# Hybrid trunk on one core: six of eight Mamba-2 groups projected in token rows, and their scans begun five steps later

## The chip, the core and the metric

The kernel runs on one core of one Trainium2 chip. The metric is the device time of one execution in microseconds. Five engines work side by side, each with its own queue in order: TensorE (PE, with its weight loads PEld) for matrix products into PSUM, VectorE (DVE), ScalarE (ACT), GpSimd (POOL), which here only issues transfers, and SyncE (SP), which issues the weight loads. PSUM is the memory that TensorE writes its sums to; SBUF is the large on-chip memory; HBM is off the chip. A partition is one of the 128 rows of SBUF or PSUM.

## The reference

One decoder layer with 256 tokens of width 2048, in float32: a token mixer of two parallel branches (HGRN2 and Mamba-2), cross-attention to 256 memory tokens, and a convolved gated feed-forward. The change lies in the Mamba-2 branch. Cut to what matters:

```python
proj = u @ w_in                        # 2048 -> z, xbc, dt and the rest
xbc = silu(causal_dwconv(xbc_raw, conv_w, conv_b))   # 4 taps over the tokens
xs, bm, cm = split(xbc)                # 2048 channels, 8 x 128, 8 x 128
dt = softplus(dt_raw + dt_bias)
y = ssd_chunk_scan(xs * dt, dt * a, bm, cm) + d_skip * xs
y = y * silu(z)                        # then an RMS norm in each of the 8 groups
y_m2 = y @ w_branch_m2
```

There are eight groups. A group has 512 channels of xbc: 256 of xs (four heads of 64), 128 of B and 128 of C. The convolution runs along the tokens, so it wants a channel in a partition and the tokens beside one another.

## The kernel before

**Weights and steps.** All weights are float32 and every product is made from two parts: a weight chunk of 1 MB (`raw`, L144, three buffers, loaded by SP in the fixed list `order`) is cast to `hi` on ScalarE (L130) and the rest `lo` is taken on VectorE (L131), in halves of 1024 columns, each with five buffers (`WB = 5`). Inputs are split in the same way; `s2` holds the mixer's normed input, 16 blocks of 128 channels, each with 256 columns of `hi` and 256 of `lo`. One call of `weights()` is one step: it lets the background work advance (`step()`), casts weights two chunks ahead, and hands out one chunk.

**Two forms of projection.** `project` makes one chunk of 128 output channels in column form, with channels in partitions: per block of input channels one product of 512 columns (`hi` weights with both parts of the input) and one of 256 (`lo` weights with the `hi` input), 32 products a step, into one PSUM tile; `join` (L263, L264) adds its two halves. `project_tok` makes 512 output channels from four chunks in token form, with tokens in partitions: two PSUM tiles, one for each 128 tokens, and 24 products of 512 columns a step; here the weights are the moving operand. There are four such PSUM tiles (`proj`).

**The Mamba-2 stage.** After the z gates and group 0 come the products of the HGRN2 branch, and then groups 1 to 7. Each even group is preceded by four steps of z gates for two groups (`m2_gates`). `m2_project(g)` makes a group's four chunks in column form, joins each into the tile `t` (one buffer) and convolves it (L725, L728) into `sz` (two buffers, shared by name with other stages). A transfer on SP brings the cumulated decays into `vc` (L718).

**The scan.** `m2_scan` is a generator in the background list; each `yield` ends its part in one step, and `pause(n)` lets n steps pass. It applies SiLU to `sz` (L740, L743), turns xs to token rows through HBM (x, into `kq`), builds the decay matrices `e0`, `e1` (L756 to L761), multiplies B and C on TensorE (`misc<-sz`) and masks them (L769, L773), scales x (L777, into `bb`), multiplies (`misc<-e,bb`), adds the skip term (L792), turns the result (`yt`, again `bb`), gates and norms it (L805 to L813), turns it back (`yc`, L817) and splits it into `ym` (L823, L828). To turn is: 32x32 transposes on VectorE (L320) into `yq` (two buffers), four transfers to HBM (L312) and one back, all issued by POOL.

**Order.** A planner orders each engine's instructions: it takes the earliest written one that it holds to be ready. Products of the background are pinned on TensorE behind what was written before them, so they come at their step; work of ScalarE and VectorE can be taken earlier than its step. A tile that has all its buffers taken waits until the last reader of the oldest is done.

**After the groups** come 16 steps of sigmoid gates (`gate`, L836, two of the four in buffers of `sz`) and the 16 steps of the branch product of `ym`, in token form; its step 4 reads groups 6 and 7.

Of the kernel before, what the change touches and what calls it, by code (L numbers as in the profile page):

```python
# [9 lines left out]
F32 = mybir.dt.float32  # L10
# [4 lines left out]
ALU = mybir.AluOpType  # L15
# [4 lines left out]
P = 128  # L20
T = 256
D = 2048
# [4 lines left out]
GROUPS = 8  # L27
# [37 lines left out]
def hybrid_trunk(ctx, tc, xT, memT, par, cst, msk, w_k0, w_ka, w_va, w_hg, w_hv, w_hog, w_ghg, w_bhg, w_dt,  # L65
# [127 lines left out]
    def pause(n):  # L193
        for _ in range(n):
            yield True
# [149 lines left out]
    def pc(name, i=0, n=1):  # L345
        o, _ = PCOLS[name]
        return par_t[:, o + i:o + i + n]
# [356 lines left out]
    def m2_chunk(g, i):  # L704
        return 2 * g + i if i < 2 else (16 + g if i == 2 else 24 + g)
# [9 lines left out]
    def m2_project(g):  # L715
        sz = mp.tile([P, 4, T], F32, name="sz", bufs=2)
        cb = mp.tile([P, 4, T], F32, name="vc", bufs=2)
        nc.sync.dma_start(out=cb, in_=cum_d[4 * g:4 * g + 4, :].partition_broadcast(P))  # L718
        for i in range(4):
            c = m2_chunk(g, i)  # L720
            ps = project(s2)
            raw = mp.tile([P, T], F32, name="t", bufs=1)
            join(mp, ps, raw)
            o = sz[:, i, :]
            V.tensor_scalar(out=o, in0=raw, scalar1=pc("m2_cw", 4 * c + 3), scalar2=pc("m2_cb", c),  # L725
                            op0=ALU.mult, op1=ALU.add)
            for s in range(1, 4):
                V.scalar_tensor_tensor(out=o[:, s:T], in0=raw[:, 0:T - s],  # L728
                                       scalar=pc("m2_cw", 4 * c + 3 - s), in1=o[:, s:T],
                                       op0=ALU.mult, op1=ALU.add)  # L730
        return sz, cb

    def m2_scan(g, sz, cb, zt):
        yield from pause(1 + 2 * (g % 2) if g else 0)

# [517 lines left out]
def _layout(inp):  # L1253
# [5 lines left out]
    swap = np.arange(D).reshape(GROUPS, 2, P // B, B).transpose(0, 2, 1, 3).ravel()  # L1259
    xs = _cols(cut(10240, 2048)).reshape(GROUPS, 2, P, 2048)  # L1260
    b = _cols(cut(12288, 1024))[:, None]
    c = _cols(cut(13312, 1024))[:, None]
    dt = np.zeros((D, P), f)
# [16 lines left out]
    def put(name, a):  # L1280
# [34 lines left out]
        "w_bhg": _toks(inp["w_branch_hg"][0]), "w_dt": _cols(dt),  # L1315
        "w_z": _toks(cut(8192, 2048)[:, swap]), "w_m2": np.concatenate([xs, b, c], 1), "w_gm2": _toks(cut(16416, 2048)),
        "w_bm2": _toks(inp["w_branch_m2"][0]), "w_out": out,
# [23 lines left out]
```

## Time and profile before

| | |
|---|---|
| median of three runs | 2229.68 us (2229.58 to 2229.78) |
| the profiled execution | 2230.02 us, its span 2228.3 us |
| granted TensorE clock | 0.998 |
| busy TensorE, VectorE, ScalarE, POOL | 100%, 74%, 59%, 8% |
| weight chunks of these groups (`raw<-in_w_m`) | 32 loads of 1 MB, 5.0 us to landing |

In the profile's rows `proj<-s,hi` is a product in column form (weights `hi` held, input `s` moving) and `proj<-hi,s` one in token form; L82 is the helper that issues them all. After `|` come busy time and mean of one, and then the engine's idle time before them and what ended it.

### The profile page before, as it was taken

The page shows a single profiled execution, that of the slowest core. Times are in us where ns is not written, and L with a number is a line of the kernel's source. Part 1 is how long each engine was busy: PE and PEld are TensorE (multiplying, and loading weights), DVE is VectorE, ACT ScalarE, POOL GpSimd, SP SyncE. Part 2 cuts the span into 40 slices and gives each one's busy share as a digit, 9 for nine tenths or more (in the row PEclk, how much of TensorE's full clock was granted, in tenths as well). Part 3 has the DMA queues.
Part 4 walks back from the last instruction along what each step waited for, and adds up shares of the span by engine and source line. Part 5 has one row for each costly group of instructions (what it writes and reads, how often), then busy time and mean ns, then how long its engine had stood idle before and what let it go on. Part 6 is the DMA issues. An engine that isn't in the chain of part 4 may idle for free.

```text
span 2228.3 us, 32921 instructions
## 1 busy us (share of the span) xinstructions
PE 2217.3 (100%) x12620; PEld 1890.7 (85%) x12620; DVE 1640.8 (74%) x2660; ACT 1321.2 (59%) x2056; POOL 186.0 (8%) x314
## 2 busy tenths in 40 slices
PE   9999999999999999999999999999999999999998
PEld 8888888888888888888888888888888888888887
DVE  8858888887645779874676766675776776699887
ACT  7567777776545577665456655554554555465554
POOL 0000100110000122220200010001000100100000
PEclk9999999999999999999999999999999999999999
DMA  8655555555655667766676654578666666655654
GB/s 307 235 187 195 184 181 181 182 186 189 228 189 201 225 234 236 229 213 219 228 247 217 219 203 174 180 226 250 214 210 211 225 214 218 213 200 211 220 205 161
DMA packets 100270, 470.45 MB, mean 211 GB/s; under 512 B 29424, under 2 KB 34064, under 8 KB 51088
## 3 DMA queue, kind: packets, MB, share of 16 engines
q1 hardware_dynamic: 69600, 432.36, 54.8%
q0 software_dynamic: 13584, 33.57, 5.3%
q10 hardware_dynamic: 16928, 2.42, 0.6%
q8 instruction: 99, 1.62, 0.3%
q14 instruction: 59, 0.48, 0.1%
HBM read 445.20 MB, written 25.20 MB: 211 GB/s over the span
## 4 chain that ended last, share of the span: by engine, by line
PE 99%; DMA 0%; ACT 0%; SPq 0%; DVE 0%; issue 0%; DVEq 0%; ACTq 0%
PE proj L82 90%; PE misc L82 5%; PE lev L82 4%; DMA raw<-in_w_k 0%; ACT misc L1204 0%; DVE h L1202 0%; PE lev L869 0%; SPq L402 0%; ACT hi L386 0%; SPq L401 0%; DVE c L1221 0%; SPq L405 0%; DVEq L1337 0%; ACT jt L263 0%; PE misc L697 0%
## 5 line engine op out<-in xcount | busy, mean ns | idle before, releaser
L131 DVE TENSOR_TENSOR lo<-raw,hi 128x1024 fp32r<-128x1024 f32 x738 | 896.5, 1222 | 458.8 <-ACT hi L130 425.9
L130 ACT CAST hi<-raw 128x1024 fp32r<-128x1024 f32 x737 | 771.9, 1051 | 546.5 <-PE proj L82 513.0
L82 PE MATMUL proj<-hi,s 128*128 128x512 f32 x2922 | 913.6, 390 | 0.0
L82 PE MATMUL proj<-s,hi 128*128 128x512 f32 x2736 | 645.1, 391 | 1.1 <-ACT hi L386 1.1
L82 PEld LDWEIGHTS proj<-hi,s 128*128 128x128 f32 x2922 | 548.4, 188 | 114.4 <-issue 0.7
L82 PEld LDWEIGHTS proj<-s,hi 128*128 128x128 f32 x2736 | 506.5, 188 | 101.8 <-ACT hi L386 1.6
L82 PE MATMUL proj<-lo,s 128*128 128x512 f32 x1461 | 568.8, 389 | 0.0
L82 PEld LDWEIGHTS proj<-s,lo 128*128 128x128 f32 x2736 | 345.3, 191 | 11.3 <-ACT s L278 0.8
L82 PE MATMUL proj<-s,lo 128*128 128x256 f32 x2736 | 351.6, 283 | 0.2 <-ACT s L278 0.2
L82 PEld LDWEIGHTS proj<-lo,s 128*128 128x128 f32 x1461 | 274.4, 188 | 55.7
L312 POOL DMA_DIRECT2D x_d<-yq x120 | 69.9, 589 | 372.2 <-DVE yq L320 365.6
L165 ACT CAST hi<-raw 128x1024 fp32r<-128x1024 f32 (+1 forms) x56 | 52.1, 944 | 55.0 <-DVE raw L174 35.1
L263 ACT COPY jt<-proj 128x256 f32<-128x256 f32 x123 | 45.6, 371 | 57.5 <-PE proj L82 56.8
L312 POOL DMA_DIRECT2D u_d<-yq x44 | 28.6, 656 | 535.9 <-DVE yq L1051 342.6
L312 POOL DMA_DIRECT2D y_d<-yq x64 | 35.1, 555 | 384.1 <-DVE sm L618 263.1
L166 DVE TENSOR_TENSOR lo<-raw,hi 128x1024 fp32r<-128x1024 f32 (+1 forms) x56 | 60.2, 1088 | 6.9 <-ACT hi L165 6.2
L1074 DVE SCALAR_TENSOR_TENSOR gc<-g,par_t,gc 128x255 f32<-128x255 f32 x88 | 42.4, 482 | 8.7 <-ACT gc L1072 6.0
L728 DVE SCALAR_TENSOR_TENSOR sz<-t,par_t,sz 128x255 f32<-128x255 f32 (+2 forms) x96 | 45.6, 475 | 1.4
L1072 ACT ACTIVATE gc<-g,par_t 128x256 f32<-128x256 f32 x44 | 26.4, 601 | 20.9 <-DVE g L1070 20.9
L82 PE MATMUL proj<-hi,ha 128*128 128x512 f32 x104 | 36.6, 389 | 0.0
L572 DVE TENSOR_TENSOR e<-e,kq 128x256 f32<-128x256 f32 x96 | 34.4, 418 | 0.0
L559 DVE TENSOR_TENSOR e<-bb 128x256 f32<-128x256 f32 x96 | 33.8, 419 | 0.1
(315 smaller groups left out, 1801.3 us busy)
## 6 DMA issues: line engine op xcount, KB each, us to landing
raw<-in_w_uv SPq DMA_DIRECT2D x44, 1024.0 KB, 4.9
raw<-in_w_ug SPq DMA_DIRECT2D x44, 1024.0 KB, 4.8
raw<-in_w_dn SPq DMA_DIRECT2D x44, 1024.0 KB, 4.8
raw<-in_w_hg SPq DMA_DIRECT2D x32, 1024.0 KB, 4.8
raw<-in_w_m SPq DMA_DIRECT2D x32, 1024.0 KB, 5.0
raw<-in_w_hv SPq DMA_DIRECT2D x16, 1024.0 KB, 4.9
raw<-in_w_hog SPq DMA_DIRECT2D x16, 1024.0 KB, 4.8
raw<-in_w_ghg SPq DMA_DIRECT2D x16, 1024.0 KB, 4.8
```

Of the source, the lines that this page charges most:

```text
L82: ins = PE.matmul(*args, **kwargs)
L130: S.copy(out=hi[:, c - a:d - a], in_=raw[:, c:d])
L131: V.tensor_tensor(out=lo[:, c - a:d - a], in0=raw[:, c:d], in1=hi[:, c - a:d - a].bitcast(F32), op=ALU.subtract)
L165: S.copy(out=hi[:, 0:d - c], in_=raw[:, c:d])
L166: V.tensor_tensor(out=lo[:, 0:d - c], in0=raw[:, c:d], in1=hi[:, 0:d - c].bitcast(F32), op=ALU.subtract)
L263: S.copy(out=tmp, in_=ps[:, T:2 * T])
L312: G.dma_start(out=yd.rearrange("(n i) (b f) -> b i n f", i=B, b=P // B)[b], in_=yq[b * B:(b + 1) * B, :].rearrange("i (n f) -> i n f", n=n))
L559: V.tensor_tensor(out=lev[hw].rearrange("p (n c i) -> p n c i", c=2, i=hw), in0=free(bb, 0, [(2 * hw, nb), (T + hw, 2), (1, hw)]), in1=fre ...
L572: V.tensor_tensor(out=ev, in0=ev, in1=free(kq, 0, [(2 * hw, nb), (T + hw, 2), (1, hw)]), op=ALU.mult)
L728: V.scalar_tensor_tensor(out=o[:, s:T], in0=raw[:, 0:T - s], scalar=pc("m2_cw", 4 * c + 3 - s), in1=o[:, s:T], op0=ALU.mult, op1=ALU.add)
L1072: S.activation(out=gc, in_=g, func=AF.Identity, bias=pc("f_cb", c), scale=pc("f_cw", 3 * c + 2))
L1074: V.scalar_tensor_tensor(out=gc[:, s:T], in0=g[:, 0:T - s], scalar=pc("f_cw", 3 * c + 2 - s), in1=gc[:, s:T], op0=ALU.mult, op1=ALU.add)
```

## The change

Groups 1 to 6 are projected in token form. Their weights are laid out for it on the host (`w_m2`, whose blocks for groups 0 and 7 stay in columns). The two PSUM tiles of a group hold 512 channels in token rows: VectorE transposes them in four operations of 128x256 straight from PSUM into `yq`, POOL sends each of two `yq` to HBM in four transfers and fetches it back in one, into `sz`, which then holds the channels in partitions but with the tokens in another order, not yet convolved. No join is made.

The convolution of these groups moves into their scan. After three steps, ScalarE copies a chunk from `sz` into `t` in the order of the tokens and VectorE convolves it back into `sz`, two chunks in the fourth step and two in the fifth; then the scan goes on with its old pause (1 step for even groups, 3 for odd ones), five steps later than it did. Group 0 is as before. Group 7 is projected as before and its scan begins three steps later (a pause of 6 for 3).

```diff
+        if 0 < g < GROUPS - 1:
+            pss = project_tok(s2)
+            for j in range(2):
+                yq = mp.tile([P, 2 * T], F32, name="yq", bufs=2)
+                for q in range(2):
+                    V.transpose(out=yq.rearrange("p (n q r) -> p q n r", q=2, r=B)[:, q],
+                                in_=pss[q][:, j * T:(j + 1) * T].rearrange("p (n c) -> p n c", c=B))
+                yd = to_squares(yq, T // B, "r_d")
+                G.dma_start(out=sz[:, 2 * j:2 * j + 2, :], in_=yd.rearrange("(i p) t -> p i t", p=P))
+            return sz, cb
         for i in range(4):
-            c = m2_chunk(g, i)
             ps = project(s2)
             raw = mp.tile([P, T], F32, name="t", bufs=1)
             join(mp, ps, raw)
-            o = sz[:, i, :]
-            V.tensor_scalar(...)
-            for s in range(1, 4):
-                V.scalar_tensor_tensor(...)
+            convolve(g, sz, i, raw)
         return sz, cb

+    def convolve(g, sz, i, raw):
+        c = m2_chunk(g, i)
+        o = sz[:, i, :]
+        V.tensor_scalar(out=o, in0=raw, scalar1=pc("m2_cw", 4 * c + 3), scalar2=pc("m2_cb", c),
+                        op0=ALU.mult, op1=ALU.add)
+        for s in range(1, 4):
+            V.scalar_tensor_tensor(out=o[:, s:T], in0=raw[:, 0:T - s],
+                                   scalar=pc("m2_cw", 4 * c + 3 - s), in1=o[:, s:T],
+                                   op0=ALU.mult, op1=ALU.add)

     def m2_scan(g, sz, cb, zt):
-        yield from pause(1 + 2 * (g % 2) if g else 0)
+        if 0 < g < GROUPS - 1:
+            yield from pause(3)
+            for i in range(4):
+                raw = mp.tile([P, T], F32, name="t", bufs=1)
+                S.copy(out=raw.rearrange("p (q b t) -> p q b t", q=2, t=B), in_=in_order(sz[:, i, :]))
+                convolve(g, sz, i, raw)
+                if i % 2:
+                    yield True
+        yield from pause((0, 1, 3, 6)[0 if g == 0 else 3 if g + 1 == GROUPS else 1 + g % 2])
...
+    xbc = np.concatenate([...], 2).reshape(D, GROUPS * 512)
+    m2 = _toks(xbc)
+    for g in (0, GROUPS - 1):
+        m2[g] = _cols(xbc[:, g * 512:(g + 1) * 512])
```

More of the change, by code (lines that the diff above doesn't have):

```diff
@@ L723, in m2_project @@
             join(mp, ps, raw)
-            o = sz[:, i, :]
-            V.tensor_scalar(out=o, in0=raw, scalar1=pc("m2_cw", 4 * c + 3), scalar2=pc("m2_cb", c),
-                            op0=ALU.mult, op1=ALU.add)
-            for s in range(1, 4):
-                V.scalar_tensor_tensor(out=o[:, s:T], in0=raw[:, 0:T - s],
-                                       scalar=pc("m2_cw", 4 * c + 3 - s), in1=o[:, s:T],
-                                       op0=ALU.mult, op1=ALU.add)
-        return sz, cb
-    def m2_scan(g, sz, cb, zt):
-        yield from pause(1 + 2 * (g % 2) if g else 0)
+            convolve(g, sz, i, raw)
+        return sz, cb
+    def convolve(g, sz, i, raw):
[7 more added lines that the diff above has]
+                                   op0=ALU.mult, op1=ALU.add)
+    def m2_scan(g, sz, cb, zt):
+        if 0 < g < GROUPS - 1:
[7 more added lines that the diff above has]
+        yield from pause((0, 1, 3, 6)[0 if g == 0 else 3 if g + 1 == GROUPS else 1 + g % 2])
         xc = mp.tile([P, 2 * T], F32, name=("w", "ql")[g % 2], bufs=1)
@@ L1259, in _layout @@
     swap = np.arange(D).reshape(GROUPS, 2, P // B, B).transpose(0, 2, 1, 3).ravel()
-    xs = _cols(cut(10240, 2048)).reshape(GROUPS, 2, P, 2048)
-    b = _cols(cut(12288, 1024))[:, None]
-    c = _cols(cut(13312, 1024))[:, None]
+    xbc = np.concatenate([cut(10240, 2048).reshape(D, GROUPS, 256),
+                          cut(12288, 1024).reshape(D, GROUPS, P),
+                          cut(13312, 1024).reshape(D, GROUPS, P)], 2).reshape(D, GROUPS * 512)
+    m2 = _toks(xbc)
+    for g in (0, GROUPS - 1):
+        m2[g] = _cols(xbc[:, g * 512:(g + 1) * 512])
     dt = np.zeros((D, P), f)
@@ L1315, in _layout @@
         "w_bhg": _toks(inp["w_branch_hg"][0]), "w_dt": _cols(dt),
-        "w_z": _toks(cut(8192, 2048)[:, swap]), "w_m2": np.concatenate([xs, b, c], 1), "w_gm2": _toks(cut(16416, 2048)),
+        "w_z": _toks(cut(8192, 2048)[:, swap]), "w_m2": m2, "w_gm2": _toks(cut(16416, 2048)),
         "w_bm2": _toks(inp["w_branch_m2"][0]), "w_out": out,
```

## The prediction

> **What bounds the kernel now.** I read the page first: the busy shares, then the chain of waits.
>
> ```profile
> span 2228.3 us, 32921 instructions
> PE 2217.3 (100%) x12620; PEld 1890.7 (85%) x12620; DVE 1640.8 (74%) x2660; ACT 1321.2 (59%) x2056; POOL 186.0 (8%) x314
> ...
> PE 99%; DMA 0%; ACT 0%; SPq 0%; DVE 0%; issue 0%; DVEq 0%; ACTq 0%
> ```
>
> TensorE is busy all the time and the chain of waits is TensorE for 99%. So a change can only gain by making TensorE's stream shorter, and can only lose by making TensorE wait. The profiled execution took 2230.02 us, the median of the runs is 2229.68, so its sum stands 0.34 us above the median.
>
> The same holds inside the stage that is changed. The view of busy time by stretches, for 71 us in its middle (columns: length, then busy time and count of PE, PEld, DVE, ACT, POOL, then clock and DMA):
>
> ```profile
> 778.00:849.00 71.00, 71.00 (x394) 60.88 (x393) 58.06 (x97) 48.85 (x80) 18.05 (x30) 1.00 0.69 232
> ```
>
> 71 us is one period of two groups: 8 steps of their own projection, 4 of the gates z, and two scans. VectorE fills 82% of it, so it has 13 us to spare in two groups and is the engine to watch.
>
> **The gain: 24 steps change their form.** A weight chunk of 1 MB is one step. In column form a step is 16 matmuls of 512 columns and 16 of 256; in token form it is 24 of 512. Both stream 12,288 columns. What a step takes is read from the timeline of PE, first over four column steps without a scan between them, then over a token stretch:
>
> ```profile
> 1150.68 7.44 PE L82 MATMUL proj<-s,hi 128*128 128x512 f32 x32
> 1157.96 4.00 PE L82 MATMUL proj<-s,lo 128*128 128x256 f32 x32
> 1161.80 7.44 PE L82 MATMUL proj<-s,hi 128*128 128x512 f32 x32
> 1169.08 4.00 PE L82 MATMUL proj<-s,lo 128*128 128x256 f32 x32
> 1172.91 2.46 PE L82 MATMUL proj<-s,hi 128*128 128x512 f32 x10
> ```
>
> ```profile
> 1040.35 0.62 PE L82 MATMUL proj<-hi,s 128*128 128x512 f32 x2
> ...
> 1041.03 0.62 PE L82 MATMUL proj<-hi,s 128*128 128x512 f32 x2
> ...
> 1082.51 0.61 PE L82 MATMUL proj<-hi,s 128*128 128x512 f32 x2
> ```
>
> Column form: 1150.68 to 1172.91 is 22.23 us for four steps, 5.558 each. Token form: three matmuls take 0.68 us (1040.35 to 1041.03), and 62 such threes lie between 1040.35 and 1082.51 (42.16 us), so eight threes take 5.440. The difference is 0.118 us, and six groups of four steps give 24 x 0.118 = 2.8 us. The reason shows in the same rows: a matmul of 512 columns comes every 7.28 / 32 = 227.5 ns and one of 256 every 3.84 / 32 = 120.0, which is 0.42 ns a column and some 12.5 ns a matmul whatever its width; token form has eight matmuls fewer per step.
>
> The Trainium skill ("TensorE: Matmul & The Clock Gate", Back-to-back issue gap) gives a warm matmul N / 2.4 + 2.5 ns. By that rule eight matmuls fewer are worth 0.02 us a step, 0.5 us in all. The rows above have five times its fixed part, and I keep to the rows.
>
> **The rest of the edit, engine by engine.** Groups of the stretch 720 to 990 us by line (busy, mean ns, idle before):
>
> ```profile
> L131 DVE TENSOR_TENSOR lo<-raw,hi 128x1024 fp32r<-128x1024 f32 x93 | 112.8, 1221 | 41.7 <-ACT hi L130 39.1 <-PE proj L82 2.2
> L130 ACT CAST hi<-raw 128x1024 fp32r<-128x1024 f32 x92 | 96.3, 1050 | 61.5 <-PE proj L82 61.2
> L312 POOL DMA_DIRECT2D x_d<-yq x84 | 49.0, 589 | 173.7 <-DVE yq L320 168.0 <-DVE sz L725 3.3 <-issue 2.4
> L728 DVE SCALAR_TENSOR_TENSOR sz<-t,par_t,sz 128x254 f32<-128x254 f32 (+2 forms) x83 | 39.3, 474 | 1.0
> L773 DVE TENSOR_TENSOR e<-e,a 128x768 f32<-128x768 f32 x13 | 12.1, 952 | 1.8 <-ACT a L771 1.8
> L264 DVE TENSOR_TENSOR t<-proj,jt 128x256 f32<-128x256 f32 x27 | 11.3, 418 | 2.0 <-ACT jt L263 2.0
> L725 DVE TENSOR_SCALAR sz<-t,par_t 128x256 f32<-128x256 f32 x27 | 11.0, 407 | 0.3
> L263 ACT COPY jt<-proj 128x256 f32<-128x256 f32 x27 | 9.9, 366 | 11.1 <-PE proj L82 11.1
> L777 DVE TENSOR_TENSOR bb<-kq,dt_tok 128x256 f32<-128x256 f32 x14 | 5.6, 417 | 5.7 <-DMA kq<-x_d 5.7
> L750 POOL DMA_DIRECT2D kq<-x_d x7 | 5.0, 721 | 29.9 <-DMA x_d<-yq 29.9
> ```
>
> The operations that this stage doesn't have are bounded by near ones, of the feed-forward part and of the scans:
>
> ```profile
> L1051 DVE STREAM_TRANSPOSE yq<-proj x22: 672/708/718, 1526.4 to 1945.0; 128x512 f32<-128x512 f32 x22
> L320 DVE STREAM_TRANSPOSE yq<-lf x16: 437/445/446, 196.3 to 562.1; 128x256 f32<-128x256 f32 x16
> L823 ACT ACTIVATE s<-yc,par_t x16: 492/495/511, 753.2 to 1027.9; 128x256 fp32r<-128x256 f32 x16
> ```
>
> VectorE, per group: out go four sums of a join, 4 x 418 = 1.7 us. In come four transposes of 128x256 out of PSUM: between half of the 708 ns of twice the width and 445 ns, I take 400, so 1.6 us. The convolutions stay, 407 + 3 x 474 = 1.83 us a chunk. ScalarE: out go four copies of 366 ns, in come four copies out of the reordered buffer, between 366 and 495 ns, I take 430: +0.3 us of some 24 a group. POOL: eight more transfers out at 589 ns and two back at 721, 6.2 us a group on top of 9 (half of the 18.05 above) in 35.5. SP's weight loads and their sizes stay. None of this lies on TensorE; the cover is the lead of the split weights. There are five buffers of half a chunk, so a half is cast when TensorE leaves the one five before it (ScalarE's 61.2 us of waiting for PE above), four halves of 2.72 us ahead of its use: 10.9 - 1.05 - 1.22 = 8.6 us of margin. A stall of ScalarE or VectorE shorter than that costs nothing; what is longer, TensorE pays.
>
> **Waits that are moved.** A scan's products are put into TensorE's order at a step; ScalarE and VectorE take the rest when the planner sees it ready. "Five steps later" thus binds the products, and the results of group 6 and 7 are needed only at the fourth step of the first branch product, 20 steps after group 7's projection, where the last scan now ends 18 steps after it (15 before). Two steps, some 11 us, are left; I cost it at nothing. On SP the transfer of a group's cumulated decays waits for the scan two groups before it, and weight loads queue behind it; such waits cost nothing so far:
>
> ```profile
> SPq L144 <- DVE lo L131: 222.1, 47, 8.8
> ...
> SPq L718 <- ACT e L758: 22.8, 5, 6.9
> ```
>
> The new wait is ScalarE's first copy, which stands in front of weight casts until the turned chunk is back from HBM. The nearest rows are two such hand-overs one behind the other on POOL, and what VectorE did at their end:
>
> ```profile
> 740.21 2.33 POOL L312 DMA_DIRECT2D x_d<-yq  x4 [9.86 <-DVE yq L320]
> 747.82 0.58 POOL L312 DMA_DIRECT2D x_d<-yq  x1 [5.28 <-DVE yq L320]
> 748.43 0.72 POOL L817 DMA_DIRECT2D yc<-x_d  x1
> ...
> 758.30 0.72 POOL L750 DMA_DIRECT2D kq<-x_d  x1 [5.62 <-DMA x_d<-yq]
> ...
> 763.28 0.76 DVE L777 TENSOR_TENSOR bb<-kq,dt_tok 128x256 f32<-128x256 f32 x2 [5.66 <-DMA kq<-x_d]
> ```
>
> A pair took 23 us from the first issue to the use, and VectorE stood 5.66 us without TensorE noticing. The copies come in at the fourth and the fifth step after the group, 3 x 5.44 = 16.3 and 21.8 us. Bounds of what the waits cost: nothing (all below 8.6 us), or, if the planner sets the copies so early that each group's wait is 9.3 us, 6 x 0.7 = 4.2 us. Nearest is the 5.66 us row, so I take nothing.
>
> Sum: 2230.02 - 2.8 = 2227.2 for a profiled execution, 2226.9 against the median; I forecast 2227.0.
>
> **Rivals.** *Late hand-over*: the 4.2 us just priced eat the gain, 2231. For it speaks the 23 us pair, against it that the steps allow nearly as much.
>
> *Group 7 blocked, slower*: the convolved buffer sz has two slots, and group 7 takes that of group 5. Group 5's products, which read it last, move from the 8th to the 13th step after its projection, while group 7 is projected, still in column form, at steps 9 to 12. Its convolutions then start together after step 13, 4 x (0.42 + 1.83) = 9.0 us on VectorE; the single buffer t, held meanwhile, keeps group 6's from running (4 x 1.83 = 7.3), and group 5's own products need 0.42 + 2 x 0.95 + 2 x 0.42 = 3.2. That is 19.5 us at one place. It costs from 8.6 us on, in so far as the planner puts it ahead of the splits, and makes the kernel slower by over 0.2% from 8.6 + 2.8 + 4.5 = 15.9 on. With 17.5 us ahead TensorE waits 8.9: 2235.8, say 2236. Whether splits get in between is seen on VectorE's timeline:
>
> ```profile
> 906.93 0.48 DVE L728 SCALAR_TENSOR_TENSOR sz<-t,par_t,sz 128x255 f32<-128x255 f32 x1
> 907.33 1.22 DVE L131 TENSOR_TENSOR lo<-raw,hi 128x1024 fp32r<-128x1024 f32 x1
> 908.46 0.48 DVE L728 SCALAR_TENSOR_TENSOR sz<-t,par_t,sz 128x254 f32<-128x254 f32 x1
> ...
> 919.82 0.95 DVE L773 TENSOR_TENSOR e<-e,a 128x768 f32<-128x768 f32 x1
> 920.69 0.47 DVE L728 SCALAR_TENSOR_TENSOR sz<-t,par_t,sz 128x254 f32<-128x254 f32 x1
> 921.08 0.95 DVE L773 TENSOR_TENSOR e<-e,a 128x768 f32<-128x768 f32 x1
> ```
>
> At 907 a split runs between two steps of a convolution, which speaks against the rival. At 920 a convolution and a scan alternate and leave no room for one, which speaks for it. While a chain of dependent operations is alone, splits get through; I count on that.
>
> *No gain*: if columns alone set the pace, a step costs the same in both forms, 2229.7. The rows of 227.5 and 120.0 ns speak against it. The skill's rule above is near this case: 2229.2.
>
> *More*: to pass 0.2%, 4.5 us, each of 24 steps would have to save 0.19 us. Only if the change removed some 2 us of small gaps in the stage too, 2224.7; the rows show no gaps that long.
>
> **Chances.** Forecast 0.57, late hand-over 0.17, group 7 blocked 0.17, no gain 0.05, more 0.04. A measurement of this kernel tells about 0.2% from no change, 2225.2 to 2234.1, so a gain of 2.8 us counts as the same: 0.57 + 0.17 + 0.05 = 0.79 same, 0.17 slower, 0.04 faster. The range goes from 2225.6, between forecast and the last case, up to 2234.0, between the two loss cases, and leaves out 0.18.
>
> **What would show it.** The two groups of PE that change, from the page:
>
> ```profile
> L82 PE MATMUL proj<-hi,s 128*128 128x512 f32 x2922 | 913.6, 390 | 0.0
> L82 PE MATMUL proj<-s,hi 128*128 128x512 f32 x2736 | 645.1, 391 | 1.1 <-ACT hi L386 1.1
> ```
>
> Right: the second falls by 384 to 2352, the first rises by 384 to 3306, 192 matmuls are fewer in all (12620 above), PE still 99% of the chain, and the stretch from the first to the last group shorter by 2.8 us. ScalarE's wait for the transfer into sz shows the hand-over, and its cost would be gaps on PE behind a weight cast, once per group. The blocked group 7 would show one gap of several us on PE, some two steps after group 5's products, with convolutions packed on VectorE ahead of it. The prediction is wrong if PE has such gaps, or if the token steps here come slower than 5.44 us.

## The result: 19.1 us slower, and the profile after

Four runs of the changed kernel gave a median of 2248.84 us (2248.52 to 2249.93), against 2229.73 (2229.58 to 2230.13) for the kernel before beside them: 1.0087 times as long (95% interval 1.0074 to 1.0099). The forecast was 2227.0 and the top of the range 2234.0. The profiled execution took 2249.93 us, its span 2248.1, 19.8 more than before.

From the page of the changed kernel:

```profile
span 2248.1 us, 32665 instructions
PE 2222.2 (99%) x12428; PEld 1883.8 (84%) x12428; DVE 1642.7 (73%) x2660; ACT 1331.4 (59%) x2062; POOL 221.8 (10%) x374
...
PE 51%; DMA 0%; issue 0%; ACT 0%; DVE 0%; DVEq 0%; POOLq 0%
...
L82 PE MATMUL proj<-hi,s 128*128 128x512 f32 x3306 | 1034.1, 391 | 3.1 <-ACT s L845 3.1
...
L82 PE MATMUL proj<-s,hi 128*128 128x512 f32 x2352 | 554.5, 390 | 4.2 <-DVE yq L725 3.2
```

The counts of matmuls are those forecast, 192 fewer, and the other engines' busy times have hardly moved (POOL's by 35.8 us). The chain of waits, TensorE for 99% before, can't be compared: here it is followed back only to 1080 us (the shares add up to 51%), and of the stage it says nothing. But the groups of PE now have idle time in front of them. The view of PE's waits says for what (columns: us in total, times, longest):

```profile
PE proj L82 <- ACT sg L712: 7.0, 1, 7.0
PE proj L82 <- DVE yq L725: 3.2, 1, 3.2
PE proj L82 <- ACT s L845: 3.1, 1, 3.1
PE misc L82 <- DVE bb L799: 1.8, 3, 1.4
```

These are 15.1 us. The three large ones have their places in PE's timeline:

```profile
919.78 0.39 PE L82 MATMUL proj<-hi,s 128*128 128x512 f32 x1
927.22 1.44 PE L82 MATMUL proj<-s,lo 128*128 128x256 f32 x5 [7.05 <-ACT sg L712]
928.67 3.07 PE L82 MATMUL misc<-e,bb 128*64 128x256 f32 x16
931.67 2.11 PE L82 MATMUL proj<-s,lo 128*128 128x256 f32 x11
933.61 0.63 PE L82 MATMUL proj<-s,hi 128*128 128x512 f32 x2
...
951.77 1.61 PE L82 MATMUL proj<-s,hi 128*128 128x512 f32 x6 [3.23 <-DVE yq L725]
...
1092.19 0.50 PE L82 MATMUL proj<-hi,s 128*128 128x512 f32 x1 [3.08 <-ACT s L845]
1092.77 0.62 PE L82 MATMUL proj<-hi,s 128*128 128x512 f32 x2
...
1097.10 0.62 PE L82 MATMUL proj<-hi,s 128*128 128x512 f32 x2
```

At 920 TensorE wants a PSUM tile for group 7's first chunk, at 948 one for its fourth, and at 1089 the results of the last scan. After the first and the last gap it is also slow for a while. From 1092.77 to 1097.10 it ran twelve matmuls of 512 columns, which at 227 ns take 2.72 us and took 4.33. From 927.22 to 933.61 it ran sixteen of 256 columns and sixteen small products of a scan in 6.39 us. At 120 ns each, and with the 1.50 us that such products took in the kernel before, that is 3.42:

```profile
922.83 1.57 PE L82 MATMUL misc<-e,bb 128*64 128x256 f32 x16
924.33 0.86 PE L82 MATMUL proj<-s,lo 128*128 128x256 f32 x5
```

The two stretches cost 1.6 and 3.0 us more. The granted clock of the changed kernel in the view by stretches confirms it (last three columns: clock, DMA share, GB/s):

```profile
919.00:932.00 13.00, 5.94 (x28) 4.66 (x27) 6.03 (x12) 9.02 (x16) 0.00 (x0) 0.64 0.37 137
...
1088.00:1098.00 10.00, 6.92 (x23) 5.23 (x23) 5.01 (x10) 2.90 (x4) 0.00 (x0) 0.83 0.47 186
```

The Trainium skill ("TensorE: Matmul & The Clock Gate", What's actually happening) halves TensorE's clock after at least one idle window of about 3.4 us and restores it after about as long a busy one. The trace agrees in the length: the second row is 17% short of 10 us, which at half speed is 3.4 us. It doesn't agree in the threshold: this came after a wait of only 3.08 us, and the 3.23 us at 948 brought none. Even 2.06 us were enough in the run with ScalarE's queue below (clock 0.86 over the 12 us from 915, again 3.4 us at half speed), and a gap of the same 2.06 us was not in the run unread through `yq` (clock 1.00 over the 12 us from 918).

So 15.1 us of waits and 4.6 of half clock, less the forecast gain of 2.8, make 16.9 of the 19.8; the 2.9 us left are in no wait that the view of the stage lists, and are not itemised here.

**What stands behind the gaps.** The PSUM tile at 920 was held by the z gates of groups 6 and 7. Their copy waits for one of the two buffers `sg`, which is free when the gate of group 3 (L827) is done; first VectorE, then ScalarE:

```profile
921.29 1.22 DVE L131 TENSOR_TENSOR lo<-raw,hi 128x1024 fp32r<-128x1024 f32 x1 [0.81 <-ACT hi L130]
922.43 0.41 DVE L740 TENSOR_SCALAR sz<-t,par_t 128x256 f32<-128x256 f32 x1
922.87 1.00 DVE L743 SCALAR_TENSOR_TENSOR sz<-t,par_t,sz 128x255 f32<-128x255 f32 x2
923.79 0.42 DVE L827 TENSOR_TENSOR kq<-bb,sg 128x256 f32<-128x256 f32 x1
...
924.52 0.42 DVE L827 TENSOR_TENSOR kq<-bb,sg 128x256 f32<-128x256 f32 x1
```

```profile
926.60 1.05 ACT L712 COPY sg<-proj 128x512 f32<-128x512 f32 x2
```

The turned result that the gate reads had been fetched by 916.3 us (issued at 912.62, 3.7 us to landing). From there to the gate VectorE was idle for 0.81 us only: it ran splits and the convolutions (L740, L743) of group 5, the late ones.

The tile at 948 was held by group 6's projection, which ended at 920, but whose second pair of transposes runs at 951:

```profile
933.22 1.30 DVE L320 STREAM_TRANSPOSE yq<-kq 128x512 f32<-128x512 f32 x2
...
943.26 0.77 DVE L725 STREAM_TRANSPOSE yq<-proj 128x256 f32<-128x256 f32 x2
951.18 0.77 DVE L725 STREAM_TRANSPOSE yq<-proj 128x256 f32<-128x256 f32 x2
```

Two turns of scans had taken both buffers `yq` at 933, and the projection's pairs came behind them, each only after POOL had sent the older content off. The other two of the four PSUM tiles were held by group 7 itself, by its second and third chunk, whose joins wait for the one buffer `t`:

```profile
938.47 0.42 DVE L264 TENSOR_TENSOR t<-proj,jt 128x256 f32<-128x256 f32 x1 [0.50 <-ACT jt L263]
...
959.90 0.41 DVE L740 TENSOR_SCALAR sz<-t,par_t 128x256 f32<-128x256 f32 x1
...
963.39 0.42 DVE L264 TENSOR_TENSOR t<-proj,jt 128x256 f32<-128x256 f32 x1
```

The first join fills `t` at 938.47. Its convolution into `sz` runs only at 959.90, behind the products of group 5 (957.4) that read the same slot of `sz`, and the second join only after that. POOL waits, in order, for the turns of both kinds (its waits in 730 to 1000 us):

```profile
POOL x_d L312 <- DVE yq L320: 77.0, 12, 16.1
POOL r_d L312 <- DVE yq L725: 42.6, 5, 26.2
POOL sz L728 <- DMA r_d<-yq: 15.8, 7, 4.5
```

The last two rows are new: for 58 us POOL stands in front of the projection's turns. In this kernel no scan's turn of the stage, once transposed, waits more than 2.0 us for its first transfer, as before; what comes late is its transpose. That scans' turns queue behind the projection's on POOL is seen with own buffers (below): a turn transposed at 850.7 us gets its first transfer at 864.8.

### The profile page after: what moved, and what is told of

Read it like the earlier page. It is cut to its first block, busy times and chain, and to the rows that moved or that the text cites. A ratio compares the mean times of both kernels' runs of the same rounds, so it can differ in the third digit from the quotient of the medians.

```text
span 2248.1 us, 32665 instructions
## 1 busy us (share of the span) xinstructions
PE 2222.2 (99%) x12428; PEld 1883.8 (84%) x12428; DVE 1642.7 (73%) x2660; ACT 1331.4 (59%) x2062; POOL 221.8 (10%) x374
## 4 chain that ended last, share of the span: by engine, by line
PE 51%; DMA 0%; issue 0%; ACT 0%; DVE 0%; DVEq 0%; POOLq 0%
PE proj L82 45%; PE misc L82 4%; PE lev L82 3%; DMA yc<-x_d 0%; ACT misc L1226 0%; PE lev L891 0%; DVE h L1224 0%; DVE c L1243 0%; DMA x_d<-yq 0%; ACT s L845 0%; DVEq L1363 0%; ACT r L1233 0%; ACT r L1234 0%; DVE r L1232 0%; POOLq L839 0%
## 5 line engine op out<-in xcount | busy, mean ns | idle before, releaser
L82 PE MATMUL proj<-hi,s 128*128 128x512 f32 x3306 | 1034.1, 391 | 3.1 <-ACT s L845 3.1
L82 PEld LDWEIGHTS proj<-hi,s 128*128 128x128 f32 x3306 | 621.2, 188 | 133.9 <-ACT s L845 3.5
L82 PE MATMUL proj<-lo,s 128*128 128x512 f32 x1653 | 645.2, 390 | 0.0
L82 PE MATMUL proj<-s,hi 128*128 128x512 f32 x2352 | 554.5, 390 | 4.2 <-DVE yq L725 3.2
L82 PEld LDWEIGHTS proj<-s,hi 128*128 128x128 f32 x2352 | 435.0, 188 | 90.8 <-issue 3.6
L82 PEld LDWEIGHTS proj<-lo,s 128*128 128x128 f32 x1653 | 310.8, 188 | 64.5 <-issue 1.5
L82 PEld LDWEIGHTS proj<-s,lo 128*128 128x128 f32 x2352 | 298.1, 192 | 17.2 <-ACT sg L712 7.5
L82 PE MATMUL proj<-s,lo 128*128 128x256 f32 x2352 | 303.8, 284 | 7.0 <-ACT sg L712 7.0
L263 ACT COPY jt<-proj 128x256 f32<-128x256 f32 x99 | 36.7, 371 | 51.2 <-PE proj L82 45.6
L743 DVE SCALAR_TENSOR_TENSOR sz<-t,par_t,sz 128x255 f32<-128x255 f32 (+2 forms) x96 | 46.0, 479 | 1.7
```

Source lines behind the costliest of these rows:

```text
L82: ins = PE.matmul(*args, **kwargs)
L263: S.copy(out=tmp, in_=ps[:, T:2 * T])
L743: V.scalar_tensor_tensor(out=o[:, s:T], in0=raw[:, 0:T - s], scalar=pc("m2_cw", 4 * c + 3 - s), in1=o[:, s:T], op0=ALU.mult, op1=ALU.add)
```

## The experiments

Differences are always to the kernel before, timed beside it (its medians lay between 2229.61 and 2230.23 us). Intervals of a ratio are some 0.1 to 0.17% to each side, 2 to 4 us.

### Which part of the change costs: form, delay, turn

*Token form alone.* Groups 1 to 6 in token form, transposed from PSUM straight into `sz`, copied and convolved at once, old pauses. The order inside a chunk's columns is then not the reference's; nothing goes through HBM.

```diff
-                yq = mp.tile([P, 2 * T], F32, name="yq", bufs=2)
                 for q in range(2):
-                    V.transpose(out=yq..., in_=pss[q][...])
-                yd = to_squares(yq, T // B, "r_d")
-                G.dma_start(out=sz[:, 2 * j:2 * j + 2, :], in_=yd...)
+                    V.transpose(out=sz[:, 2 * j + q, :]..., in_=pss[q][...])
...
-            yield from pause(3)
-                if i % 2:
-                    yield True
-        yield from pause((0, 1, 3, 6)[...])
+        yield from pause((0, 1, 3, 3)[...])
```

> Groups 1 to 6 in token form, but their chunks are transposed from PSUM straight into the convolved buffer (32x32 blocks, so the values are in wrong places), without yq, without POOL and HBM; the convolutions follow the projection and all scans keep the old pauses. It leaves out the turn and the delay. Both theories (turns, delay) expect the bare gain of the matmul form: 2.8 us, 2226.9, and no gap on PE over 0.5 us. If it stays at 2229.7 the forecast's gain itself was wrong.

Measured 2233.49 us, +3.9 (ratio 1.0016, 1.0007 to 1.0026), with one gap of 2.9 us in front of a scan's products: a miss for both theories. Why the form alone costs was not followed up.

*Delay alone.* The kernel before, in column form, its scans five steps later (group 7's three).

```diff
-        yield from pause(1 + 2 * (g % 2) if g else 0)
+        yield from pause((0, 6, 8, 6)[0 if g == 0 else 3 if g + 1 == GROUPS else 1 + g % 2])
```

> The kernel before with only the pauses changed: scans of groups 1 to 6 five steps later, that of group 7 three; column form, no added turn. Delay theory (tiles live five steps longer, so the z gates of groups 6 and 7 find no buffer and hold PSUM): slower by 10 to 20 us, 2240 to 2250, with the gap of some 7 us on PE ahead of group 7's first chunk. Turn theory (the added turns fill yq's two buffers and POOL's queue): 2229.7 within 2 us.

Measured 2231.43 us, +1.8 (1.0006 to 1.0025), no gap of a microsecond in the stage of the profiled execution (2230.89 us). Four of the ten runs took 2233.94 to 2240.19 us.

*Form and delay, no turn.* The first kernel with the changed kernel's pauses and with its copies and convolutions in the scan.

> Token form and the changed kernel's pauses, copies and convolutions, but no turn of the projected chunks: VectorE transposes them straight from PSUM into sz, without yq, POOL or HBM (values in wrong places). It leaves out 60 transfers. If the turns are what costs (run with turns and old pauses: 2237; delay alone in column form: 2231), this is the gain with next to nothing taken off: 2227 to 2229, PE gaps below 2 us in all. If token form and delay together are enough, without any turn: 2238 or more.

Measured 2230.01 us, +0.3 (0.9992 to 1.001). Both parts together cost less than the form alone; from the delay alone they can't be told apart. All but 0.3 of the 19.1 us, give or take 2, hang on the way through `yq`, POOL and HBM.

*The turn without the delay.* The first kernel, with the projection also transposed into `yq` and sent to HBM in its 48 transfers, which nobody reads; the copies that are used still go straight into `sz`.

```diff
+                yq = mp.tile([P, 2 * T], F32, name="yq", bufs=2)
+                for q in range(2):
+                    V.transpose(out=yq..., in_=pss[q][...])
+                to_squares(yq, T // B, "r_d")
```

> As the run without turns, but the added transposes into yq and the eight transfers of a group to HBM are made as well (48 transfers in all; they are not read back, and the values stay in wrong places); old pauses. It leaves out the twelve transfers back and the delay. Turn theory: yq and POOL alone put the scans late, 2232 to 2245, with gaps on PE. Delay theory: 2227 to 2228, since VectorE has 1.6 us more per group and nothing else.

Measured 2237.24 us, +7.6 (1.0022 to 1.0048), 3.8 more than without it: sending, with its second transposes into `yq`, costs before anyone waits for it.

### Two remedies, and why they don't add up

*Own buffers.* The turned projections take a tile of `vc`, the buffers of the cumulated decays, which are fetched later, after the convolutions; everything stays on POOL.

```diff
+            yp = mp.tile([P, 4, T], F32, name="vc", bufs=2)
             for j in range(2):
-                yq = mp.tile([P, 2 * T], F32, name="yq", bufs=2)
+                yq = yp[:, 2 * j:2 * j + 2, :].rearrange("p a t -> p (a t)")
```

> The changed kernel, whole, but the projected chunks are transposed into a buffer of the ring vc (4 KB, which the group's decays took at that time; those are now fetched in the scan, after the convolutions) and not into yq's two. Turn theory with yq as the narrow place: the transposes of groups 5 and 6 come right behind their projection, not 14 and 23 us later, and the time falls to 2227 to 2234. Delay theory, or POOL's queue as the narrow place: 2245 to 2250, the gaps stay.

Measured 2240.60 us, +11.0 (1.0028 to 1.0058), between the two expectations: 8.1 of the 19.1 us are back.

*Another queue.* `yq` shared as in the changed kernel, the projection's 60 transfers on SP instead of POOL.

```diff
-                yd = to_squares(yq, T // B, "r_d")
-                G.dma_start(out=sz[...], in_=...)
+                yd = to_squares(yq, T // B, "r_d", nc.sync)
+                nc.sync.dma_start(out=sz[...], in_=...)
```

> The changed kernel with the projected chunks' 60 transfers issued by SP instead of POOL; yq stays shared with two buffers. POOL's order as the cause: transfers of the scans no longer stand behind those of the projection, 2230 to 2237, gate of group 3 back near its step. yq's two buffers as the cause: little changes, 2243 to 2250.

Measured 2240.17 us, +10.4 (1.003 to 1.006), between the two expectations again.

*Both.*

> Both remedies: the projected chunks are transposed into a buffer of vc and sent by SP. If yq and POOL together are the cause, only the lateness of the last scan stays: 2228 to 2233. If something else (kq, bb, sg, held five steps longer) is, it stays near 2240.

Measured 2244.51 us, +14.8 (1.0049 to 1.0083), worse than either. PE's and SP's waits with both remedies:

```profile
PE proj L82 <- ACT hi L130: 9.2, 2, 5.0
```

```profile
SPq L312 <- DVE vc L728: 31.8, 6, 10.8
```

SP runs ahead of TensorE, so it reaches a group's transfers before the transposes are done; the weight loads stand behind it for up to 10.8 us, and TensorE waits twice for a cast, 4.2 and 5.0 us.

*Both, the transfers written one step later.* They move from the projection into the scan, behind a `pause(1)`.

> The changed kernel with a buffer of its own for the turned projections (as in the run with own buffers, the cumulated decays fetched later) and with their transfers on SP, but written into SP's order one step later than in the run where both remedies gave 2244.5 us: there SP waited 32 us for the transposes (SPq L312 <- DVE vc) and weight loads behind it came late (5 us gaps on PE that ended with a weight cast). Theory 'queues and buffers': the loss is time in which something else stands behind a waiting transfer; one step later the transposes are done, SP doesn't wait for them (under 5 us in all), no weight is late, POOL has its old list, and the time comes to 2230 to 2234 us, near the 2230.0 of the run with no turn through HBM; what may remain is the last scan's end (up to 3 us). Rival 'traffic': the 60 transfers themselves slow down the others on the DMA rings wherever they are issued; then it stays at 2238 us or more with hand-overs of the scans as late as in the changed kernel.

Measured 2249.49 us, +19.3 (1.007 to 1.0104). SP's wait for the transposes stayed at 32.4 us, since the planner put the transfers in front of the same weight loads as before; the run decides nothing on the two theories.

*Own buffers, ScalarE's queue.* The 60 transfers are issued by ScalarE.

> The changed kernel with a buffer of its own for the turned projections and their 60 transfers issued by ScalarE right behind the transposes. Theory 'queues and buffers': neither POOL's list of turns nor SP's list of weights stands behind them; ScalarE waits for the HBM writes in front of a fetch (12 times 2 to 3 us), below the 8.6 us margin of the weight casts, so 2230 to 2236 us. Rival 'traffic': 2238 us or more, as with any other queue. [...]

Measured 2243.33 us, +13.1 (1.0045 to 1.0075), as the rival "traffic" has it and a miss for the theory of queues and buffers. ScalarE's queue was not free of charge: each of the 48 transfers out took it 0.49 us to issue (median). PE's waits were short and many, for weights' low parts (3.0 us), masks (2.8) and the join (1.2).

*Both, three steps later.* One more weight load stands ahead of each group's transfers.

```diff
-            yield from pause(3)
+            yield from pause(3)
+            for j in range(2):
+                yq = cb[:, 2 * j:2 * j + 2, :].rearrange("p a t -> p (a t)")
+                yd = to_squares(yq, T // B, "r_d", nc.sync)
+                nc.sync.dma_start(out=sz[:, 2 * j:2 * j + 2, :], in_=yd...)
+            yield True
             for i in range(4):
...
-                if i % 2:
-                    yield True
+            cb = decays(g)
+            yield True
```

> The changed kernel with own buffers and the transfers on SP, written three steps later than in the run of 2244.5 us and with all four copies in one step behind them, so that the scans stay where they are. In the run with one step SP took the transfers no later than before, in front of the same weight loads, and waited for the transposes as long (32 us), which is why its 2249.5 us decided nothing. Here one more weight load stands ahead of each group's transfers. Theory 'a waiting transfer holds up what stands behind it': SP's wait for the transposes (SPq L312 <- DVE vc) falls to under 10 us, gaps of PE behind weight casts go, and the time falls to 2231 to 2238 us. Rival 'the turned chunk is too late for its convolution' gets worse, as the chunk comes some 5 us later: 2245 us or more, with ScalarE's copies waiting for sz<-r_d.

Measured 2241.90 us, +12.0 (1.0034 to 1.0068). SP's wait went as foreseen and the 5 us gaps behind weight casts are gone. SP's and PE's waits:

```profile
SPq L312 <- DVE vc L728: 2.8, 4, 1.0
```

```profile
PE proj L82 <- ACT s L852: 3.4, 1, 3.4
PE misc L82 <- DVE bb L806: 2.5, 1, 2.5
```

Yet the time is 2241.9, not the 2231 to 2238 expected: now the scans are late, the last one by 3.4 us. What SP changed beside the order is the packets. The same 48 transfers, in the view of DMA of 730 to 960 us, own buffers on POOL, then on SP:

```profile
DMA packets 11650, 56.73 MB, mean 247 GB/s; under 512 B 2716, under 2 KB 2716, under 8 KB 6753
...
raw<-in_w_z SPq DMA_DIRECT2D x9, 1024.0 KB, 5.2
```

```profile
DMA packets 25747, 57.44 MB, mean 250 GB/s; under 512 B 15089, under 2 KB 18161, under 8 KB 20866
...
raw<-in_w_z SPq DMA_DIRECT2D x9, 1024.0 KB, 7.0
```

There are 12,373 more packets under 512 B, 258 a transfer of 64 KB, so about one for each run of 256 B; from POOL they left in larger ones. The z weights land in 7.0 us instead of 5.2, the groups' own in 5.2 instead of 5.4. The Trainium skill ("DMA: Bandwidth & Descriptors", SWDGE vs HWDGE vs iDMA) sends plain transfers to the queues of SP or ACT. Here that gained 8.7 us with `yq` shared; with own buffers the four runs on SP or ScalarE stand 1.0 to 8.3 us above the one on POOL, of which the 1.0 can't be told from no change. How much of SP's 2241.9 is packets and how much order was not separated.

### A turn that nobody reads: four kernels, two causes

*Unread, from `sz`.* The kernel with form and delay and no turn, with the 60 transfers put back on POOL: each half of `sz` goes to HBM right after its transposes and on to a second HBM buffer. POOL's list of work is nearly that of the run with own buffers.

```diff
+                yq = sz[:, 2 * j:2 * j + 2, :].rearrange("p a t -> p (a t)")
+                yd = to_squares(yq, T // B, "r_d")
+                yr = dp.tile([P, 2, T], F32, name="q_d", bufs=4)
+                G.dma_start(out=yr, in_=yd.rearrange("(i p) t -> p i t", p=P))
```

> The run without the turn (transposes from PSUM straight into sz, the changed kernel's pauses, copies and convolutions; it measured 2230.0 us) with the turn's 60 transfers put back on POOL: each half of sz is sent to HBM in four transfers right after its transposes and on to a second HBM buffer in a fifth. Nobody reads what they bring, and no buffer yq is taken, so the projection waits for nothing new; but POOL's list of work is the one of the run with own buffers (2240.6 us), with the scans' own turns standing behind the transfers of the projected chunks, and the traffic is the same. It leaves out the use of the turned chunk. Theory 'POOL's order': scans' turns come late because POOL waits, in order, for the transposes and for the way back of projected chunks; then the loss stays without any consumer: 2237 to 2241 us, products that wait for e or bb and a late last scan on PE. Theory 'consumer': what costs is that convolutions get their chunk late and push ScalarE and VectorE work together; then it is 2230 to 2232 us, with POOL's waits as long but no gap on PE.

Measured 2233.40 us, +3.5 (1.0007 to 1.0026), between the two expectations and nearer to the second. POOL's longer list and the traffic cost 3.2 us over the kernel without a turn. So the rival "traffic", by which the 60 transfers cost wherever they are issued, is worth no more than that on POOL.

*Unread, through `yq`.* The same with the shared buffers: VectorE transposes a second time, into `yq`, and POOL sends that. POOL's list is then exactly the changed kernel's; VectorE has four more transposes a group.

> The run with the unread turn (2233.4 us) with the turn put back into the shared buffers yq: VectorE transposes each half a second time, from PSUM into yq, and POOL sends yq instead of sz; POOL's list of work is then exactly that of the changed kernel. The chunk that is used still goes from PSUM straight into sz, so nothing reads what the turn brings (it leaves out the use of the turned chunk, and VectorE does four more transposes a group, some 1.7 us). Theory 'yq costs by itself': the transposes wait for a yq that a scan's turn holds, VectorE and the PSUM tiles are held with them, and the loss is the difference between the changed kernel and the run with own buffers, 8 us, on top of 2233.4: 2239 to 2243 us, with transposes of group 4 and 6 tens of us after their projection and one PE gap in front of group 7 or of the z gates. Theory 'only together': a late transpose costs because the convolution behind it is late; without that reader it is 2233 to 2236 us.

Measured 2241.73 us, +11.5 (1.0037 to 1.0071), as the theory "`yq` costs by itself" has it. With the run with own buffers and the changed kernel this makes a table (us above the kernel before):

| | turned chunk not read | turned chunk read |
|---|---|---|
| no shared `yq` | 3.5 | 11.0 |
| shared `yq` | 11.5 | 19.1 |

`yq` costs 8.0 or 8.1 us, reading costs 7.5 or 7.6, whichever way one goes. The two add up within the intervals; that they do so to 0.1 us is luck. The rows differ in a little more than `yq`: with it and unread, VectorE transposes twice, and in the run with own buffers the decays are fetched later.

### Why does reading cost 7.5 us?

Not by ScalarE's wait for it. The 24 copies of the changed kernel (L752) and what ScalarE waited for before them:

```profile
L752 ACT COPY t<-sz x24: 398/406/412, 746.7 to 990.3; 128x256 f32<-128x256 f32 x24
...
  DVE sz L743: 11.5, 12
  DMA sz<-r_d: 2.3, 1
```

*A second guess: the buffer `bb`.* In all runs with the turn each scaling of x, into the one buffer `bb`, follows the gate of the scan before, which frees it. Three kernels fetch `yt` into `yc` (two buffers) instead: with own buffers, the changed kernel, and the kernel before.

```diff
-        yt = mp.tile([P, 2, T], F32, name="bb", bufs=1)
+        yt = mp.tile([P, 2, T], F32, name="yc", bufs=2)
```

> The run with own buffers for the projected turns (2240.6 us) with one more edit: the turned result yt of a scan is fetched into yc (two buffers) instead of bb (one), so that the next scan's scaled x, which is also called bb, doesn't have to wait for the gate of the scan before. In the traces bb is held from the scaling of x to the gate for 26 to 29 us of a group's 35.5 in the kernel before, for 27 to 45 us with own buffers, and there each scaling of x follows the gate before it by 2 to 6 us. Theory 'the one bb is where late turns add up': the scans then overlap, a late gate holds up no next scan, the 7.2 us that reading the turned chunk costs shrink to 3 or less, 2233 to 2237 us, and the last scan is no longer late on PE. Rival 'the late convolutions themselves': nothing changes by more than 2 us, 2238.5 us or more; masks and scaled x are as late as before because VectorE does the convolutions first.

> The changed kernel with yt in yc instead of bb, and nothing else. By the theory 'the one bb', late gates no longer hold up the next scan, but the projected chunks still wait for a shared yq, so the 8 us of yq stay and the 7 us of reading shrink: 2240 to 2244 us. By the rival it stays within 2 us of 2248.8.

> The kernel before with yt in yc instead of bb: what the exchange of the buffer does by itself, where bb has 7 to 9 us to spare in each group. Both theories expect no change, 2229 to 2231 us; a loss here would have to be added to what the other two runs with this edit show.

Measured 2240.44, 2248.49 and 2230.49 us, where 2240.60, 2248.84 and 2230.11 stand without it. The theory falls. In the second of them the 7.0 us behind `sg` are gone, and at the same 920 us PE waits 5.2 for the scaled x instead:

```profile
PE misc L82 <- DVE bb L799: 5.2, 1, 5.2
PE proj L82 <- ACT s L845: 3.6, 1, 3.6
PE proj L82 <- DVE yq L725: 3.2, 1, 3.2
```

One late thing gives way to the next: the gap's releaser names who came last, not the cause.

*A third: the date of the convolutions.* The unread kernel, with its copies held at the step where they are written instead of as soon as the chunk is there.

```diff
-                S.copy(out=raw..., in_=in_order(sz[:, i, :]))
+                tc.keep_in_program_order(S.copy(out=raw..., in_=in_order(sz[:, i, :])))
```

> The run with the unread turn (2233.4 us: the chunk goes from PSUM straight into sz, the 60 transfers on POOL are read by nobody) with ScalarE's 24 copies out of sz held at the place where they are written, the fourth and fifth step after the group, instead of as soon as the chunk is there. In the run where the turned chunk is read (2240.6) the first copies of groups 1 to 6 start 6 to 21 us later than in the unread run. It leaves out the use of the turned chunk as that run does. Theory 'late convolutions': it is the date of the convolutions that costs, because they then stand on VectorE beside a scan's masks, scaling and gate; with late copies and nothing read, the 7.2 us come back, 2238 to 2242 us. Rival 'the transfer back': the loss hangs on the chunk's way through HBM itself (a late landing in a single place); then late copies cost little, 2233 to 2236 us.

Measured 2240.61 us, +10.4 (1.0028 to 1.0062): 6.9 of the 7.5 us are back, with nothing read. The copies are later here, though, than where the chunk is read: group 4's first stands at 885.0 us, with own buffers at 871.5, unread at 850.4. So late copies are enough to cost as much; that reading costs by its date alone is likely, but not shown.

*Late copies with no turn at all.* The same edit in the kernel with form and delay, which sends nothing for the projected chunks.

> The run without the turn (2230.0 us) with ScalarE's 24 copies held at their written place, the fourth and fifth step after the group; nothing is sent to HBM for the projected chunks (their 60 transfers are left out, as in that run). Theory 'late convolutions by themselves': VectorE is crowded at the late date whatever POOL does, so most of the 7.2 us come back here too, 2235 to 2238 us. Rival 'late convolutions behind late turns': they cost only where the scans' own turns are already behind on POOL, and with POOL's old list the scans still have time: 2230 to 2232.5 us.

Measured 2228.98 us, -1.2 (0.9986 to 1.0005): no cost, and the lowest time of this study, though not told from no change. Group 4's first copies in the unread, the unread late and the last kernel:

```profile
850.44 0.40 ACT L753 COPY t<-sz 128x256 f32<-128x256 f32 x1
```

```profile
884.99 0.39 ACT L753 COPY t<-sz 128x256 f32<-128x256 f32 x1
```

```profile
864.58 0.39 ACT L749 COPY t<-sz 128x256 f32<-128x256 f32 x1
```

So late convolutions cost only where POOL also carries the projection's turns: with POOL's old list the copy held at its step comes at 865, with the longer list the same code comes to it at 885. What of POOL's part is its order and what the traffic was not separated, and more buffers `yq` were not tried. No kernel of the study is faster than the kernel before by more than a measurement can tell.

## Why the prediction was wrong

**Right: the gain on TensorE.** In the changed kernel, an undisturbed stretch of token steps:

```profile
846.40 0.62 PE L82 MATMUL proj<-hi,s 128*128 128x512 f32 x2
...
870.20 0.62 PE L82 MATMUL proj<-hi,s 128*128 128x512 f32 x2
```

35 threes lie between the rows, 23.80 / 35 = 0.680 us each and 5.440 a step, as forecast. The rule of the Trainium skill ("TensorE: Matmul & The Clock Gate", Back-to-back issue gap), by which a step saves 0.02 us, doesn't hold here: it saves 5.558 less 5.440. But the 2.8 us were never measured whole: without the turn the time was +0.3 and -1.2 us, give or take 2, so that only the second leaves room for them. In the first of these group 7 waits 1.3 us for its join, in the second no wait above 0.2 us is left in the stage.

**Right: the prices of single operations.** Copies of 406 ns (430 taken), transposes of 408 (400), POOL's busy time up by 35.8 us, 6.0 a group (6.2).

**Wrong: "none of this lies on TensorE".** This is the step that failed. It priced the four transposes and ten transfers of a group as engine time, and held them against one margin, the 8.6 us lead of the split weights. What they take is not time but places: two buffers `yq` that served three turns a group and now serve five, four PSUM tiles that stay held until the transposes get a `yq`, and POOL's list, in which a scan's turn stands behind the projection's (with own buffers up to 14.1 us). `yq` costs 8 us, POOL's list and its traffic 3 us, and reading the turned chunk, most likely by the late convolutions, 7.5 us. None of the three passes through the split weights: in the changed kernel no wait of PE that the view of the stage lists ends with them.

**Right in words, wrong in use: the new wait.** The copy's wait for the transfer was taken at nothing and measures 2.3 us in all. Its price, though, was looked for in that wait; it lay in what comes later because of it.

**Wrong: "two steps, some 11 us, are left; I cost it at nothing".** The last scan's split, in the kernel before and in the kernel without turn and with late copies (ScalarE), and the gap at the product that reads it, in the unread kernel (PE):

```profile
1027.50 0.91 ACT L823 ACTIVATE s<-yc,par_t 128x256 fp32r<-128x256 f32 x2 [1.30 <-DMA yc<-x_d]
```

```profile
1071.87 0.91 ACT L842 ACTIVATE s<-yc,par_t 128x256 fp32r<-128x256 f32 x2 [0.90 <-DMA yc<-x_d]
```

```profile
1075.08 0.50 PE L82 MATMUL proj<-hi,s 128*128 128x512 f32 x1 [1.63 <-ACT s L846]
```

The split moved by 44 us, not by three steps, even in the best kernel, and with the product due at about 1073.5 (1075.08 less the 1.63 us) nothing was left. In the changed kernel it was 3.08 us late, plus 1.6 of half clock. The products of the last scan had moved by 34.7 us themselves (993.38 before, 1028.05 in the best kernel): right before them its scaled x waits for the gate of group 6, which frees the one `bb`. That isn't all: with own buffers and `yc` for `bb` the products come at 1013.9, 22.0 us earlier than with own buffers alone, and the split only 5.6. What else holds the end of the scans was not followed up.

**The rivals.** "Group 7 blocked" named the place, one gap of several us at group 7, and gave 2236. Its mechanism is in the trace: group 7's first convolution waits for the products of group 5, and `t` and two PSUM tiles with it, at the gap of 3.23 us, which a late `yq` ended. The longer gap, 7.05 us, ended with the copy of the z gates, held by `sg`; convolutions were packed on VectorE ahead of it, as the rival says, but group 5's, ahead of a gate. The blocking alone costs nothing: in the best kernel group 7's first join and its convolution stand as far apart (926.76 and 942.71 us), and PE waits for neither. "Late hand-over" had the turned chunk as the late thing, but priced at 4.2 us what cost 7.5. No rival had POOL's queue or the buffers `yq`, which the scans' turns share, so the range ended 14.8 us short. By the prediction's own chances the range leaves out 0.17 + 0.04 = 0.21, not 0.18.

## What to carry to other kernels

A transfer or a transpose on an idle engine is not free: count who else uses its buffers and what stands behind it in its queue, and for how long each use holds them. Where a small ring already serves several stages, five users for three was a slowdown here with POOL 10% busy. To find the cause of scattered gaps, don't follow the releaser of each; put the suspected work in without its reader, and the reader's delay in without the work.

## What was not expected of the hardware

Half clock came after gaps as short as 2.06 us, though not after each, and made a gap of the changed kernel cost about half as much again: 1.6 us on 3.08, and 3.0 on 7.05. A transfer out of 256-byte runs leaves POOL's queue in larger packets and SP's in about one for each run. And some of these kernels scatter, for a reason that no run shows: with own buffers and `yc`, four runs lay between 2236.58 and 2242.94 us, and with the delay alone, without any turn, ten between 2230.38 and 2240.19, where the kernel before has 2229.65 to 2230.75.
